# A Hymba block with PEER experts: the squares of the attention summed block by block, the conv squares added before one product, two 1/rms on quarters of the tokens

## The chip, the core and the metric

The kernel runs on one core of one Trainium2 chip. A core has a matrix engine (TensorE, PE), a vector engine (VectorE, DVE), a scalar engine (ScalarE, ACT), a general engine (GpSimd, POOL) and SyncE (SP), whose queue issues most DMA transfers. Each engine works through its own list of instructions in a fixed order; semaphores hold an instruction back until what it needs is done. The metric is the device time of one execution in microseconds (us), the median of several runs.

## The reference

One decoder layer over 512 tokens of width 1024, cut to what matters here:

```python
mod = c_act @ ada_w + ada_b                  # shift1, scale1, gate1, shift2, scale2, gate2
h = modulate(rmsnorm(x, norm1_g), shift1, scale1)
q, k, v, cb, cc, cu = split(h @ w_in)
attn = sliding_window_attention(rope(rmsnorm(q)), rope(rmsnorm(k)), v, sinks)   # 8 heads of 64
conv = cb * short_conv(cc * cu, conv_w)                                         # 512 channels
merged = concatenate([rmsnorm(attn, attn_out_g), rmsnorm(conv, conv_out_g)])
x = x + gate1 * (merged @ w_out)
h2 = modulate(rmsnorm(x, norm2_g), shift2, scale2)
x = x + gate2 * peer(h2, wq, subkeys, u, v)  # 16 queries per token, top 16 of 128 x 128 keys, 16384 experts
```

Each rmsnorm divides by the root of the mean square over the channels of one token. There are three such norms of whole rows that matter here: of the attention output (512 channels), of the conv output (512 channels), and of the new x ahead of PEER (1024 channels).

## The kernel before

Activations lie transposed: channels on the 128 partitions, in 8 chunks of 128, and the 512 tokens along the row. A product in full precision is made of three fast ones: each operand is split into a rounded part and a rest (`split`, lines 174 to 177: ACT copies the rounded part, hi, and DVE subtracts it for the rest, lo), and `mm3` (lines 197 to 202) multiplies hi by hi, hi by the activations' rest, and lo by hi. A block of 128 output channels over 1024 inputs is 24 products of 128x128 by 128x512.

The stages follow each other: the first norm and the modulation weights (0 to 60 us in the trace), the input projection with the attention and conv woven in (60 to 166), the rest of the attention (to 187), the output projection (to 231), the second norm and the first queries (to 254), the other queries (to 345), their routing and the table of the dense experts (to 640), and the experts themselves (to the end). PEER handles most tokens densely, with all 16384 expert rows streamed through, and the last ones by gathers of rows.

The order of the second stage is written out by hand in the string PLAN: A0 to A3 are the scores and softmax of four blocks of 128 tokens (`attend1`, line 374), B0 to B3 their second halves (`attend2`, lines 408 to 434: per head a transpose of the probabilities on PE, line 416, a copy pT on ACT, line 418, the products po, line 425; at the end of the block one copy into attnT, line 434), C30 to C32 the three projections of a conv chunk (lines 438 to 452), S the squares of the conv output summed by PE against a matrix of ones (lines 234 to 237), N the conv half of the merged norm (`part_norm`, lines 463 to 468: f is the scaled chunk on DVE, mH and mL its two parts), M two loads of modulation weights. The end of PLAN is "C31 C32 S B2 N B3 M M M". Behind it come the squares of attnT (ssa), the first half of the output projection for four blocks (py, over the conv half), the attention half of the norm, and the rest of the projection. A scheduler places the instructions on each engine, in about this order but by its own estimates of when they are ready.

Three details are needed below. A sum against ones gives the same sum on all 128 partitions, as a 128x512 tile in PSUM; `rstd` (lines 239 to 243) takes its root on ACT and the reciprocal on DVE, both 128x512. Modulation weights (`ada`, lines 204 to 214) are loaded into two buffers, each load held back until a mark on PE, and each multiplied and summed by one DVE instruction (junk, line 213). Temporary tiles come from one pool, tp, with nine buffers (line 107).

After the projection, `spill` (lines 528 to 536) transposes the new x by token (xt, 32 transposes on PE), copies it (xn on ACT, from pool rt with three buffers), and stores it to DRAM (x1s). The second norm's sums (ss2, lines 550 to 552) are one product over seven added squares and one over the eighth. The first two queries (pq) follow each chunk of the normed fH and fL (lines 226 to 232). Then pools are closed, and `query` (lines 721 to 732) loads its keys sk over SP's queue, into a pool opened on memory that tp gave back, and `scores` (lines 734 to 745) multiplies query and keys (psc).

Of the kernel before, what the change touches and what calls it, by code (L numbers as in the profile page):

```python
# [7 lines left out]
F32 = mybir.dt.float32  # L8
# [10 lines left out]
P = 128  # L19
# [70 lines left out]
def body(tc, p):  # L90
# [13 lines left out]
    rt, rt_s = pool("rt", side="right")  # L104
    R2 = dict(tag="s2", bufs=3)
    tp, tp_s = pool("tp", side="right")
    T2 = dict(tag="t2", bufs=9)
    xp, xp_s = pool("xp", side="right")

    def bank(name):  # L110
        return psm.tile([P, 512], F32, tag="m", name=name)
# [104 lines left out]
    def tmp(name):  # L216
        return tp.tile([P, T], F32, name=name, **T2)

    def squared(b, so_far=None):
        q = tmp("sq")  # L220
        nc.scalar.activation(q, b, AF.Square)
        if so_far is not None:
            nc.vector.tensor_add(q, q, so_far)
        return q
# [9 lines left out]
    def square(ps, b, i, n, w=None):  # L234
        q = tmp("sq")
        nc.scalar.activation(q, b, AF.Square)
        nc.tensor.matmul(ps, ones if w is None else w, q, start=(i == 0), stop=(i == n - 1))

    def rstd(ps, n):
        r = tmp("rstd")  # L240
        nc.scalar.activation(r, ps, AF.Sqrt, scale=1.0 / n, bias=eps)
        nc.vector.reciprocal(r, r)
        return r
# [130 lines left out]
    def attend1(n):  # L374
        k0 = 0 if n else P
        s = a1.tile([P, 8, 256], F32, tag="s", name="s", bufs=2)
        for b2 in range(2):
            pss = [bank("sc") for g in range(2)]
            for i in range(2):
                b = 2 * b2 + i  # L380
                for g, ps in enumerate(pss):
                    gp = slice(64 * g, 64 * g + 64)
                    nc.tensor.matmul(ps[:, i * 256 + k0:(i + 1) * 256], qT[gp, b, n * P:(n + 1) * P],
                                     kT[gp, (n - 1) * P + k0:(n + 1) * P], start=True, stop=True)
            for g, ps in enumerate(pss):
                for i in range(2):
                    h = 4 * g + 2 * b2 + i
                    nc.vector.scalar_tensor_tensor(s[:, h, k0:], ps[:, i * 256 + k0:(i + 1) * 256], rq[:, n, h:h + 1],
                                                   mask[:, k0:], op0=OP.mult, op1=OP.add)
        m = a1.tile([P, 8], F32, name="m", bufs=2)  # L390
        nc.vector.reduce_max(m, s[:, :, k0:], axis=X)
        nc.vector.tensor_max(m, m, S("sink"))
        nm = a1.tile([P, 8], F32, name="nm", bufs=2)
        nc.vector.tensor_scalar_mul(nm, m, -1.0)
        den = a1.tile([P, 8], F32, name="den", bufs=2)
        for h in range(8):
            nc.scalar.activation(s[:, h, k0:], s[:, h, k0:], AF.Exp, bias=nm[:, h:h + 1],
                                 accum_out=den[:, h:h + 1])
        es_ = a1.tile([P, 8], F32, name="es_", bufs=2)
        nc.vector.tensor_add(es_, S("sink"), nm)  # L400
        nc.scalar.activation(es_, es_, AF.Exp)
        nc.vector.tensor_add(den, den, es_)
        nc.vector.reciprocal(den, den)
        for h in range(8):
            nc.vector.tensor_scalar_mul(s[:, h, k0:], s[:, h, k0:], den[:, h:h + 1])
        return s
# [53 lines left out]
    vT = tmp("vT")  # L460
    nc.scalar.activation(vT, pj[5], AF.Copy)
    kg = S("kg")
    def part_norm(ss, src, g, o):
        r = rstd(ss, 512)
        for k in range(4):
            f = tmp("f")
            nc.vector.scalar_tensor_tensor(f, src[:, k, :], S(g, k), r, op0=OP.mult, op1=OP.mult)
            split(mH[:, o + k, :], mL[:, o + k, :], f)
# [4 lines left out]
    def out_half(b, half):  # L473
        if half == 0:
            wo[b] = weights_of(p["w_out"][b])
            py[b] = bank("py")
        mm3(py[b], wo[b], mh, ml, range(4 * half, 4 * half + 4))
# [3 lines left out]
    for step in PLAN.split():  # L481
        n = [int(x) for x in step[1:]]
        match step[0]:
            case "k":
                nk = qk1(pj[4], qk0(pj[4]), kg)
            case "q":
                nq[n[0]] = q0(pj[n[0]], n[0])
            case "P":
                pj[n[0]] = proj(n[0])
            case "V":  # L490
                pt = bank("vt")
                for c in range(NCH):
                    nc.tensor.transpose(pt[:, c * P:(c + 1) * P], vT[:, c * P:(c + 1) * P], ident)
                nc.scalar.activation(vN.rearrange("p a b -> p (a b)"), pt, AF.Copy)
            case "r":
                qk2(nq.pop(n[0]), qT[:, n[0], :])
            case "R":
                qk2(nk, kT)
            case "T":
                nc.scalar.activation(rq, ssq, AF.Sqrt, bias=eps64)  # L500
                nc.vector.reciprocal(rq, rq)
            case "A":
                sa[n[0]] = attend1(n[0])
            case "B":
                attend2(n[0], sa[n[0]])
            case "C":
                conv(*n)
            case "M":
                more_ada()
            case "S":  # L510
                ssc = bank("ssc")
                for k in range(4):
                    square(ssc, convT[:, k, :], k, 4)
            case "N":
                mH = a1.tile([P, DC, T], F32R, tag="hH", name="mH")
                mL = a1.tile([P, DC, T], F32R, tag="hL", name="mL")
                part_norm(ssc, convT, "cg", 0)
    ssa = bank("ssa")
    for k in range(4):
        square(ssa, attnT[:, k, :], k, 4)  # L520
    for b in range(HEAD):
        out_half(b, 0)
    part_norm(ssa, attnT, "ag", 4)
    ab = S("ada_b")
    nc.vector.tensor_add(mod[:, 16:24], mod[:, 16:24], ab[:, 16:24])
    x1s = dp.tile([NCH, P, D], F32, name="x1s")
# [1 line left out]
    def spill(half, when):  # L528
        for c in range(NCH):
            ps = bank("xt")  # L530
            for i in range(4):
                after(nc.tensor.transpose(ps[:, i * P:(i + 1) * P], xT[:, 4 * half + i, c * P:(c + 1) * P], ident),
                      when)
            xn = rt.tile([P, 512], F32, name="xn", **R2)
            nc.scalar.activation(xn, ps, AF.Copy)
            nc.sync.dma_start(x1s[c][:, half * 512:(half + 1) * 512], xn)

# [10 lines left out]
        if b < 6:  # L548
            more_ada(3)
    sq = squared(xT[:, 6, :], sq)  # L550
    nc.tensor.matmul(ss2, ones, sq, start=True, stop=False)
    end = nc.tensor.matmul(ss2, ones, squared(xT[:, 7, :]), start=False, stop=True)
    nc.vector.tensor_add(mod[:, 24:48], mod[:, 24:48], ab[:, 24:48])
    nc.vector.scalar_tensor_tensor(s2, mod[:, 32:40], 1.0, S("n2g"), op0=OP.add, op1=OP.mult)
    a1_s.close()
# [16 lines left out]
    hx, hx_s = pool("hx")  # L572
    fH = hx.tile([P, DC, T], F32R, name="fH")
    fL = hx.tile([P, DC, T], F32R, name="fL")
    r2 = rstd(ss2, D)
    spill(0, end)
    spill(1, end)
    early = [(weights_of(p["wq"][b]), bank("pq")) for b in range(EARLY)]
    fs = []
# [552 lines left out]
```

## Time and profile before

| | |
|---|---|
| three runs, us | 1436.77, 1436.56, 1435.25; median 1436.56 |
| the profiled execution, us | 1436.58 |
| its span in the trace, us | 1434.8 |
| PE busy | 1385.5 us, 97% of the span |
| DVE busy | 1229.3 us, 86% |
| ACT busy | 616.0 us, 43% |
| POOL busy | 442.7 us, 31% |
| mean granted clock of PE | 0.994 |

Times in the trace count from the start of the span. A row of the timeline has the start, the time from there to the end of the last of the group, the engine, the line of the kernel, the operation, out<-in, the shape and how many; in brackets stands the idle time just before it and what ended it. A fp32 product counts as two records. A line of the windows has the busy time of each engine in a stretch. "SPq" is a transfer's issue on SP's queue, not the transfer.

### The profile page before, as it was taken

To read this page: it belongs to the slowest core of one execution; us is meant where nothing else is said; L and a number is where in the kernel's file an instruction comes from. 1 tells how busy PE (TensorE), PEld (TensorE's weight loads), DVE (VectorE), ACT (ScalarE), POOL (GpSimd) and SP (SyncE) were. 2 spreads that over 40 slices of the span, in tenths; PEclk is the share of its full clock that TensorE was granted. 3 is DMA by queue.
4 is the path that set the end of the run, shared out by engine and by line. 5 is a ranking of instruction groups with operands and counts; after the bars stand their busy time and mean duration, and the time that the engine had idled before them with its cause. 6 is when DMAs were issued, how large, how long until landed. Compare 5 with 4: busy or idle time off the path is not lost.

```text
span 1434.8 us, 21241 instructions
## 1 busy us (share of the span) xinstructions
PE 1385.5 (97%) x7696; PEld 1218.7 (85%) x7696; DVE 1229.3 (86%) x2253; ACT 616.0 (43%) x1041; POOL 442.7 (31%) x306
## 2 busy tenths in 40 slices
PE   6999998999997999999999999999999999999998
PEld 4676776888997999999888888889999998889997
DVE  7778988789999999997668989888889979898964
ACT  4524645544634556463433333333344324333431
POOL 0000001440112320510134444456556556565400
PEclk9999999999999999999999999999999999999999
DMA  8645545322687997998999999999999999999843
GB/s 282 213 150 195 190 131 197 99 86 78 212 290 236 383 372 262 348 356 324 365 333 374 405 396 379 396 370 360 360 362 396 383 357 343 367 339 390 318 147 132
DMA packets 134376, 418.80 MB, mean 292 GB/s; under 512 B 12800, under 2 KB 39552, under 8 KB 132736
## 3 DMA queue, kind: packets, MB, share of 16 engines
q1 hardware_dynamic: 92800, 266.45, 51.6%
q0 software_dynamic: 41472, 151.01, 27.9%
q8 instruction: 60, 0.98, 0.3%
q14 instruction: 44, 0.36, 0.1%
HBM read 375.77 MB, written 41.62 MB: 291 GB/s over the span
## 4 chain that ended last, share of the span: by engine, by line
PE 62%; DVE 20%; DMA 8%; issue 7%; POOL 1%; ACT 1%; SPq 0%; DVEq 0%; POOLq 0%; ACTq 0%
PE o L997 10%; PE o L998 10%; PE o L996 10%; PE pa L200 5%; PE pa L202 5%; PE pa L201 5%; DVE lo L177 4%; DMA row<-in_vL,eG 3%; DMA ada<-in_ada 2%; PE pq L202 2%; PE pq L201 2%; PE pq L200 2%; DVE B L946 2%; DVE ga L912 2%; PE pj L200 2%
## 5 line engine op out<-in xcount | busy, mean ns | idle before, releaser
L176 ACT ACTIVATE hi<-raw 128x1024 fp32r<-128x1024 f32 x298 | 312.1, 1053 | 286.8 <-issue 91.4
L177 DVE TENSOR_TENSOR lo<-raw,hi 128x1024 fp32r<-128x1024 f32 x284 | 345.2, 1218 | 31.9 <-ACT hi L176 31.1
L202 PE MATMUL pa<-h2H,lo 128*128 128x352 f32 x1024 | 329.8, 322 | 5.6 <-DVE lo L177 5.5
L200 PE MATMUL pa<-h2H,hi 128*128 128x352 f32 x1024 | 332.3, 325 | 2.2 <-ACT sp L620 2.2
L201 PE MATMUL pa<-h2L,hi 128*128 128x352 f32 x1024 | 328.9, 321 | 0.0
L997 PE MATMUL o<-lo,wwh 128*128 128x512 f32 x768 | 299.2, 390 | 0.9 <-DVE lo L177 0.9
L996 PE MATMUL o<-hi,wwh 128*128 128x512 f32 x768 | 299.6, 390 | 0.0
L998 PE MATMUL o<-hi,wwl 128*128 128x512 f32 x768 | 298.8, 389 | 0.0
L776 POOL DMA_INDIRECT row<-in_uR,eG x128 | 186.7, 1459 | 321.3 <-PE o L998 187.8
L776 POOL DMA_INDIRECT row<-in_vL,eG x128 | 178.8, 1397 | 136.8 <-PE o L998 65.6
L784 DVE SCALAR_TENSOR_TENSOR junk<-row,h2N 128x1024 bf16<-128x1024 f32 x128 | 153.8, 1220 | 64.9 <-DMA row<-in_uR,eG 64.4
L202 PEld LDWEIGHTS pa<-h2H,lo 128*128 128x128 f32 x1024 | 192.7, 188 | 6.9 <-DVE lo L177 6.8
L200 PEld LDWEIGHTS pa<-h2H,hi 128*128 128x128 f32 x1024 | 192.2, 188 | 4.9 <-ACT sp L620 2.7
L201 PEld LDWEIGHTS pa<-h2L,hi 128*128 128x128 f32 x1024 | 192.5, 188 | 2.2
L912 DVE SCALAR_TENSOR_TENSOR ga<-row,av,ga 128x1024 f32<-128x1024 f32 x127 | 162.8, 1282 | 29.8 <-DMA row<-in_vL,eG 28.7
L998 PEld LDWEIGHTS o<-hi,wwl 128*128 128x128 f32 x768 | 144.2, 188 | 30.0
L997 PEld LDWEIGHTS o<-lo,wwh 128*128 128x128 f32 x768 | 144.2, 188 | 29.7 <-DVE lo L177 1.6
L996 PEld LDWEIGHTS o<-hi,wwh 128*128 128x128 f32 x768 | 144.2, 188 | 28.3 <-issue 0.2
L176 ACT ACTIVATE wwh<-w 128x768 fp32r<-128x768 f32 x64 | 54.1, 846 | 168.0 <-DVE w L979 120.8
L177 POOL TENSOR_TENSOR lo<-raw,hi 128x1024 fp32r<-128x1024 f32 x14 | 33.8, 2413 | 288.3 <-ACT hi L176 288.3
L978 ACT ACTIVATE w<-G 128x32 f32<-128x32 f32 x128 | 22.3, 221 | 191.3 <-DVE wwl L177 182.8
L776 POOL DMA_INDIRECT row<-in_uR,eH x32 | 43.2, 1350 | 161.7 <-DVE junk L784 74.5
(266 smaller groups left out, 1896.1 us busy)
## 6 DMA issues: line engine op xcount, KB each, us to landing
raw<-in_uL SPq DMA_DIRECT2D x128, 512.0 KB, 6.0
raw<-in_vL SPq DMA_DIRECT2D x128, 512.0 KB, 6.5
Gd<-st SPq DMA_DIRECT2D x12, 2048.0 KB, 10.2
G<-Gd SPq DMA_DIRECT2D x16, 1536.0 KB, 12.5
ada<-in_ada SPq DMA_DIRECT2D x32, 512.0 KB, 4.3
Ad<-sp SPq DMA_DIRECT2D x34, 352.0 KB, 6.5
sp<-Ad SPq DMA_DIRECT2D x34, 352.0 KB, 6.6
raw<-in_w_in SPq DMA_DIRECT2D x18, 512.0 KB, 5.2
```

Of the source, the lines that this page charges most:

```text
L176: nc.scalar.activation(h, f, AF.Copy)
L177: by.tensor_sub(l, f, h.bitcast(F32))
L200: nc.tensor.matmul(ps, wh(k), rh(k), start=(k == k0), stop=False)
L201: nc.tensor.matmul(ps, wh(k), rl(k), start=False, stop=False)
L202: mark[0] = nc.tensor.matmul(ps, wl(k), rh(k), start=False, stop=(k == k1))
L776: d = nc.gpsimd.indirect_dma_start(out=t, out_offset=None, in_=tab, in_offset=bass.IndirectOffsetOnAxis(ap=e, axis=0))
L784: return nc.vector.scalar_tensor_tensor(junk, t, 1.0, h, op0=OP.mult, op1=OP.mult, accum_out=a)
L912: nc.vector.scalar_tensor_tensor(ga, t, av[:, k:k + 1], ga, op0=OP.mult, op1=OP.add)
L946: nc.vector.tensor_mul(B.rearrange("p t (h a b) -> p t h a b", h=8, a=4), H[:, ts, :, None, :].to_broadcast(sh), L[:, ts, None].to_broadca ...
L996: nc.tensor.matmul(o, wh[:, cs], vh[:, hs], start=(j == 0), stop=False)
L997: nc.tensor.matmul(o, wh[:, cs], vl[:, hs], start=False, stop=False)
L998: last = nc.tensor.matmul(o, wl[:, cs], vh[:, hs], start=False, stop=(j == NJ - 1))
```

## The change

Four things change.

- **The attention's squares.** As soon as the copy of a token block into attnT is there, its squares are taken (`attn_squares`) and summed by four products with 32 columns of ones into 32 partitions: block 0 and 1 after A3, block 2 in step N, ahead of the conv norm, and block 3 behind the first half of block 0 of the output projection. The root and the reciprocal are then taken on a 128x128 tile (four groups of 32 partitions, one for each block of 128 tokens; `grouped_root`), and `spread` brings the result back to 128x512 with four products.
- **The conv squares** are added on DVE first, and one product sums them.
- **The second norm** has its sums in the same grouped form: two times four products, a 128x128 root and reciprocal, and `spread` between the two halves of the transposes.
- **Buffers.** tp has 13 buffers where it had 9, and xn comes from it.

```diff
-    T2 = dict(tag="t2", bufs=9)
+    T2 = dict(tag="t2", bufs=13)
...
+    def grouped(ps, q, first, last):
+        for c in range(NCH):
+            end = nc.tensor.matmul(ps[32 * c:32 * c + 32, 0:P], ones[:, 0:32], q[:, c * P:(c + 1) * P], start=first,
+                                   stop=last)
+        return end
+    def grouped_root(ps, n):
+        r = cp.tile([P, P], F32, tag="r", name="r", bufs=1)
+        nc.scalar.activation(r, ps[:, 0:P], AF.Sqrt, scale=1.0 / n, bias=eps)
+        nc.vector.reciprocal(r, r)
+        return r
+    def spread(r):
+        ps = psa.tile([P, 512], F32, tag="a", name="rr")
+        for c in range(NCH):
+            nc.tensor.matmul(ps[:, c * P:(c + 1) * P], ident[:, 32 * c:32 * c + 1].to_broadcast([P, P]), r,
+                             start=True, stop=True)
+        return ps
...
+    def attn_squares(n):
+        if n == 0:
+            ssa.append(psa.tile([P, 512], F32, tag="a", name="ssa"))
+        q = tmp("sq").rearrange("p (k t) -> p k t", k=4)
+        nc.scalar.activation(q, attnT[:, :, n * P:(n + 1) * P], AF.Square)
+        for k in range(4):
+            nc.tensor.matmul(ssa[0][32 * n:32 * n + 32, 0:P], ones[:, 0:32], q[:, k], start=(k == 0), stop=(k == 3))
...
             case "A":
                 sa[n[0]] = attend1(n[0])
+                if n[0] == NCH - 1:
+                    for c in range(NCH - 2):
+                        attn_squares(c)
...
             case "S":
                 ssc = bank("ssc")
+                q = None
                 for k in range(4):
-                    square(ssc, convT[:, k, :], k, 4)
+                    q = squared(convT[:, k, :], q)
+                nc.tensor.matmul(ssc, ones, q, start=True, stop=True)
             case "N":
...
-                part_norm(ssc, convT, "cg", 0)
-    ssa = bank("ssa")
-    for k in range(4):
-        square(ssa, attnT[:, k, :], k, 4)
-    for b in range(HEAD):
+                attn_squares(NCH - 2)
+                part_norm(rstd(ssc, 512), convT, "cg", 0)
+    out_half(0, 0)
+    attn_squares(NCH - 1)
+    ra = grouped_root(ssa[0], 512)
+    for b in range(1, HEAD):
         out_half(b, 0)
-    part_norm(ssa, attnT, "ag", 4)
+        if b == 1:
+            ra = spread(ra)
+    part_norm(ra, attnT, "ag", 4)
...
-            xn = rt.tile([P, 512], F32, name="xn", **R2)
+            xn = tmp("xn")
...
-    nc.tensor.matmul(ss2, ones, sq, start=True, stop=False)
-    end = nc.tensor.matmul(ss2, ones, squared(xT[:, 7, :]), start=False, stop=True)
+    grouped(ss2, sq, True, False)
+    end = grouped(ss2, squared(xT[:, 7, :]), False, True)
...
-    r2 = rstd(ss2, D)
+    r2 = grouped_root(ss2, D)
     spill(0, end)
+    r2 = spread(r2)
     spill(1, end)
```

What the scheduler makes of it is seen in the order of each engine. On DVE, ahead of the output projection, before (convT is the last conv chunk, lo the rest of a weight block, junk the modulation weights, rstd the reciprocal of the conv norm, f its first scaled chunks):

```order
L177 TENSOR_TENSOR lo<-raw,hi 128x1024
L452 TENSOR_TENSOR convT<-pj,y 128x512
L177 TENSOR_TENSOR lo<-raw,hi 128x1024
L213 SCALAR_TENSOR_TENSOR junk,mod<-ada,cact 128x1024 x2
L242 RECIPROCAL rstd<-rstd 128x512
L213 SCALAR_TENSOR_TENSOR junk,mod<-ada,cact 128x1024
L467 SCALAR_TENSOR_TENSOR f<-convT,sm,rstd 128x512 x3
```

and now, where sq<-sq adds the squares of the conv chunks:

```order
L223 TENSOR_TENSOR sq<-sq 128x512
L473 TENSOR_TENSOR convT<-pj,y 128x512
L223 TENSOR_TENSOR sq<-sq 128x512
L177 TENSOR_TENSOR lo<-raw,hi 128x1024
L223 TENSOR_TENSOR sq<-sq 128x512
L213 SCALAR_TENSOR_TENSOR junk,mod<-ada,cact 128x1024
L177 TENSOR_TENSOR lo<-raw,hi 128x1024
L213 SCALAR_TENSOR_TENSOR junk,mod<-ada,cact 128x1024 x4
L263 RECIPROCAL rstd<-rstd 128x512
L213 SCALAR_TENSOR_TENSOR junk,mod<-ada,cact 128x1024
L498 SCALAR_TENSOR_TENSOR f<-convT,sm,rstd 128x512 x3
```

The reciprocal of the conv norm stood behind two junk operations and now stands behind five; the last sum of squares stands behind a weight split. On ACT at the same place, before (pT are the copies of the transposed probabilities, the first eight of block B2, and rstd<-ssc the root of the conv norm):

```order
L236 ACTIVATE sq<-convT 128x512
L418 ACTIVATE pT<-pT 128x256 x3
L241 ACT_TABLE_LOAD
L241 ACTIVATE rstd<-ssc,eps 128x512
L418 ACTIVATE pT<-pT 128x256 x5
L434 ACTIVATE attnT<-po 128x4x128
```

and now:

```order
L221 ACTIVATE sq<-convT 128x512
L439 ACTIVATE pT<-pT 128x256 x8
L455 ACTIVATE attnT<-po 128x4x128
L439 ACTIVATE pT<-pT 128x256
L491 ACTIVATE sq<-attnT 128x512
L262 ACT_TABLE_LOAD
L262 ACTIVATE rstd<-ssc,eps 128x512
```

The root moved from behind the third pT copy of B2 to behind all of B2, one copy of B3 and the square of token block 2. On SP's queue, between the stores of x1 and the queries, before (x1s<-xn stores x1, sk are the keys of a query, raw<-in_wq a block of query weights):

```order
L536 DMA x1s<-xn 128x512 x8
L729 DMA sk<-in_sk 128x128 x3
L181 DMA raw<-in_wq 128x1024
L729 DMA sk<-in_sk 128x128
L181 DMA raw<-in_wq 128x1024
```

and now:

```order
L575 DMA x1s<-xn 128x512 x8
L181 DMA raw<-in_wq 128x1024
L769 DMA sk<-in_sk 128x128 x3
L181 DMA raw<-in_wq 128x1024
L769 DMA sk<-in_sk 128x128 x2
```

A load of query weights moved ahead of the first three loads of keys. It waits for POOL's split (lo) of an earlier block, before as now. The first sk load now also waits for the seven other transfers' queues, for DVE and for PE, since its buffer lies on memory that tp's larger ring held; before, it waited for DVE, PE and one transfer's queue.

On PE, eight of the small products for the squares now stand ahead of the last conv chunk's projection; the single product of the conv squares stands ahead of B2's transposes; the squares of the last token block stand behind block 0's first half of the output projection, the four products of `spread` behind block 1's; and in the second norm the order is 16 transposes, four products of `spread`, 16 transposes. On ACT all eight xn copies now stand ahead of the first fH; before, five did. The scores of query 0 stand ahead of the products of the third query, before as now.

More of the change, by code (lines that the diff above doesn't have):

```diff
@@ L462, in body, with part_norm @@
     kg = S("kg")
-    def part_norm(ss, src, g, o):
-        r = rstd(ss, 512)
+    ssa = []
+    def attn_squares(n):
[5 more added lines that the diff above has]
+            nc.tensor.matmul(ssa[0][32 * n:32 * n + 32, 0:P], ones[:, 0:32], q[:, k], start=(k == 0), stop=(k == 3))
+    def part_norm(r, src, g, o):
         for k in range(4):
```

## The prediction

> **What bounds the kernel now.** I read the page first, for the span, and then the busy times by window, for the stages that the change touches and two behind them. Their columns are the window, its length, busy time and instructions of TensorE (PE), of its weight loads, of VectorE (DVE), ScalarE (ACT) and GpSimd (POOL), the granted TensorE clock, and the DMA share.
>
> ```profile
> span 1434.8 us, 21241 instructions
> ...
> 166.00:187.00 21.00, 17.30 (x113) 10.28 (x113) 18.64 (x27) 13.84 (x30) 0.00 (x0) 1.00 0.61 201
> ...
> 187.00:231.00 44.00, 44.00 (x194) 36.05 (x192) 36.40 (x49) 14.46 (x18) 2.60 (x1) 1.00 0.51 165
> ...
> 254.00:345.00 91.00, 91.00 (x464) 77.01 (x462) 79.93 (x496) 37.74 (x78) 28.43 (x12) 1.00 0.32 97
> ...
> 400.00:640.00 240.00, 229.06 (x1894) 224.97 (x1894) 239.44 (x469) 122.61 (x212) 60.90 (x40) 0.99 0.88 322
> ```
>
> The output projection (187 to 231) and the queries (254 to 345) leave PE no gap; from 400 to 640 DVE has none (239.44 of 240). So a delay at 187 or at 254 should travel whole to the end. What can be won or lost lies between: 3.7 us without PE in 166 to 187, and the second norm after 231. The PE timeline shows who ends those gaps.
>
> ```profile
> 136.81 1.09 PE L416 MATMUL pT<-cst,s 128*128 128x128 f32 x8
> ...
> 142.40 2.00 PE L383 MATMUL sc<-kT,qT 64*128 64x256 f32 x16
> ...
> 166.06 0.39 PE L202 MATMUL pj<-hH,lo 128*128 128x512 f32 x1
> ...
> 179.38 1.31 PE L425 MATMUL po<-pT,vN 128*64 128x128 f32 x16
> ...
> 183.50 1.98 PE L237 MATMUL ssa<-sq,ones 128*128 128x512 f32 x4 [2.80 <-ACT sq L236]
> 185.77 1.98 PE L237 MATMUL ssa<-sq,ones 128*128 128x512 f32 x4 [0.29 <-ACT sq L236]
> 187.19 0.80 PE L200 MATMUL py<-mH,hi 128*128 128x512 f32 x1
> ...
> 230.93 0.39 PE L202 MATMUL py<-mH,lo 128*128 128x512 f32 x1
> ```
>
> The in-projection ends at 166.45. Before py, PE has 2.80 + 0.29 us idle, waiting for the attention's last copy and squares, and four long products; the conv norm (mH) is ready by then. This is what the change is aimed at. Block B1 takes 5.6 us of PE (136.81 to 142.40). From 187.19 to 230.93 a product starts every (43.74 - 0.64)/190 = 0.227 us.
>
> **The change, part by part: up to the output projection.** The small products have no row of their own. The nearest are po (16 records, eight products, 1.31 us: 0.16 each) and psc (in the fence on the tail; four products, the next one starts 0.82 later: 0.21 each). I take 0.2, with 0.15 as the lower end. Eight of them now stand ahead of the last four projection blocks, which so end at 166.45 + 1.6 = 168.1.
>
> ```profile
> 173.11 1.23 DVE L213 SCALAR_TENSOR_TENSOR junk<-ada,cact 128x1024 bf16<-128x1024 f32 x1 [2.35 <-DMA ada<-in_ada]
> 175.48 3.35 DVE L242 RECIPROCAL rstd<-rstd 128x512 f32<-128x512 f32 x1
> ...
> 179.99 2.07 DVE L467 SCALAR_TENSOR_TENSOR f<-convT,sm,rstd 128x512 f32<-128x512 f32 x3
> 181.98 1.89 DVE L177 TENSOR_TENSOR mL<-f,mH 128x512 fp32r<-128x512 f32 x3
> ```
>
> The conv squares are now added on DVE, three adds of about 0.65 (the time of mL or f), and one product follows the last add. In the new order that add stands behind the last convT and one weight split: 168.1, convT and an add to 169.6, the split (1.23 on the same width) and an add to 171.4. B2's transposes stand behind that product on PE, so PE idles from 168.1 to 171.4, 3.3 us; it runs the product to 172.3, and B2 to 177.9.
>
> On ACT the root of the conv norm now stands behind eight pT copies, attnT, another pT and a square of attnT:
>
> ```profile
> 171.13 1.28 ACT L241 ACT_TABLE_LOAD   x1
> ...
> 176.10 1.21 ACT L418 ACTIVATE pT<-pT 128x256 f32<-128x256 f32 x4
> ```
>
> pT is 0.3 each, attnT and a square 0.6 each, the table load 1.28: 177.9 + 0.6 + 0.3 + 0.6 + 1.3 + 0.6 puts the root at 181.2. Two later pT copies wait behind it, so B3 ends near 185.
>
> The reciprocal meets a longer wait on DVE, since five junk operations (products with the modulation weights, ada) stand ahead of it where two stood. ada has two buffers, so each load is issued after the junk two before it. The landing times of the two loads at 166.5 and of the three from 174.4:
>
> ```profile
> L211 SPq DMA_DIRECT2D ada<-in_ada x2: 327/379/431, 166.5 to 166.8; - x2
> ...
> DMA to landing us min/median/max: 6.6/7.0/7.5
> ```
> ```profile
> L211 SPq DMA_DIRECT2D ada<-in_ada x3: 327/328/328, 174.4 to 180.1; - x3
> ...
> DMA to landing us min/median/max: 3.4/4.4/4.8
> ```
>
> The first pair waits for the last projection product, 168.1, as it did at 166.48. I give the first load 3.4 (the weight loads ahead of it have 1.6 us more to clear), the next 4.4, the third 3.4. First load lands at 171.5, its junk ends at 172.8; the third load of the stage goes out at 172.9, lands at 177.3, junk to 178.5; the fifth goes out at 178.6, lands at 182.0, junk to 183.2. Then the reciprocal, 3.35, to 186.6, one more junk to 187.8, the first f to 188.5 and mH (some 0.65) to 189.1. So py starts near 189.2, with PE idle for about 4 us after B3. The first block is then paced by DVE: f x3 and mL x3 to 191.8, f, mH and mL to 193.6; 179 products remain at 0.227 (40.6), and eight small ones for the last squares and the spread of 1/rms (1.6). The last py starts at 235.8 against 230.93: **+4.9**. With all loads at 3.4 and 0.15 a small product it is +3.1; with 6.6, 4.8 and 4.4 it is +9.5.
>
> [...]
>
> **The change, part by part: the tail.** Times here are in before's frame, without the 4.9.
>
> ```profile
> 234.08 1.12 PE L552 MATMUL ss<-sq,ones 128*128 128x512 f32 x2 [0.20 <-ACT sq L221]
> 235.04 3.66 PE L532 MATMUL xt<-cst,xT 128*128 128x128 f32 x32
> ...
> 241.74 0.73 PE L200 MATMUL pq<-fH,hi 128*128 128x512 f32 x2 [3.04 <-ACT fH L230]
> ...
> 253.19 1.91 PE L593 MATMUL pg<-cst,f 128*128 128x128 f32 x16
> 254.93 1.06 PE L738 MATMUL psc<-sk,qs 128*128 128x128 f32 x8
> ```
> ```profile
> 235.96 3.35 DVE L242 RECIPROCAL rstd<-rstd 128x512 f32<-128x512 f32 x1 [2.45 <-ACT rstd L241]
> ```
> ```profile
> 240.97 0.71 ACT L230 ACTIVATE fH<-f,mod 128x512 fp32r<-128x512 f32 x1
> ```
>
> A 128x128 reciprocal is no row; by width it is 3.35/4 = 0.84, with the full 3.35 as the other end. Grouped products end at 234.9, root 235.3, reciprocal 236.2, ready before half the xt transposes are through (236.9). The four spreading products (0.8) then fill PE till 237.5, and the other half runs to 239.4. But ACT now copies all eight xn before the first fH, and the last xn ends at about 239.95; fH starts at 240.0 against 240.97, and the first queries come some 1.1 earlier: pq's last product ends near 252 where it ended at 253.19. With the full 3.35 the spread waits until 238.7 and this 1.1 is gone.
>
> What is late next is the key load sk of query 0. The larger tmp pool pushes the pool that holds sk down onto buffers of tmp, so sk now waits for their last readers, the last of them PE's pg transposes; and on SP's queue the load of in_wq, which waits for POOL's lo, stands ahead of it.
>
> ```profile
> 253.60 2.37 POOL L177 TENSOR_TENSOR lo<-raw,hi 128x1024 fp32r<-128x1024 f32 x1 [18.26 <-ACT hi L176]
> ```
> ```profile
> 249.27 1.28 SPq L729 DMA_DIRECT2D sk<-in_sk  x3
> ...
> 256.00 0.33 SPq L181 DMA_DIRECT2D raw<-in_wq  x1
> ```
> ```profile
> L729 SPq DMA_DIRECT2D sk<-in_sk x10: 328/328/423, 249.3 to 294.4; - x10
> ...
> DMA to landing us min/median/max: 1.7/1.8/3.3
> ```
>
> These are ten sk loads. The 3.3 belongs to the one issued at 256.43, right behind the load of in_wq at 256.00; that is where the first will now stand, so I take it, and 1.7 as the other end. Before, sk went out at 249.27, 5.7 us before psc. Now: POOL's lo 1.1 earlier, in_wq out at 254.9, sk at 255.3, landed at 258.6; psc, which stands ahead of the third query's products on PE, starts at 258.7 against 254.93: **+3.7**, with PE idle 5.0 us. If sk lands in 1.7 it is +2.1.
>
> **The clock.** The gaps of 2.80 and 3.04 us above left the granted clock at 1.00. The one longer gap in the first part of the dense build:
>
> ```profile
> 444.66 0.27 PE L954 MATMUL gps<-B,A 128*128 128x128 f16 x1 [6.99 <-DVE B L946]
> ```
> ```profile
> 441.00:442.00 1.00, 0.00 (x0) 0.85 0.53 57
> ...
> 447.00:448.00 1.00, 1.00 (x13) 0.50 0.36 61
> 448.00:449.00 1.00, 1.00 (x13) 0.73 0.75 213
> ```
>
> It fell about 4.2 us into the gap (0.50 from about 441.8) and came back near 448.5, so 3.8 us of work ran at half, at most 1.9 lost. The gap of 5.0 us before psc is longer than 4.2, the other two are not. I take half of it, **+0.9**, with 0 and 1.9 as ends. [...]
>
> **Sum.** 4.9 + 3.7 + 0.9 = +9.5 on the profiled execution. That took 1436.58, 1.78 around its span of 1434.8, and is the median of the runs shown: 1446.1. The ends of the terms give 3.1 + 2.1 = 5.2 (1441.8) and 9.5 + 3.7 + 1.9 = 15.1 (1451.7).
>
> **The rivals.** *More lost:* the clock falls after all three new gaps (3.3, 4 and 5.0). For it: all three are longer than any that kept the clock. Against: the fall came 4.2 into the gap. Three times 1.9 on 8.6 is 14.3: 1450.9.
>
> *The lost time is made up later, so no slower.* DVE sets the pace from 400 to 640, and has 11 us free from 254 to 345. If its work there keeps its old pace and only PE's start slips, PE's delay is taken out of the 11 us that PE idles in the dense build. Deciding point: whether the last DVE operation before 345 starts later. Then all but about 0.5 returns: 1437. Against: DVE's work there follows each psc.
>
> *The saving comes through, so faster.* If the ada weights land early enough that the reciprocal has ended when B3 ends (reciprocal started by 181.8 at the latest), py starts at 185.2, 2.0 earlier, less 1.6 for the eight small products; the tail's 1.1 comes on top if sk is not late: 1435.1; a little more if the small products take 0.15, and a first block without pauses. Against: three chained loads that each take at least 3.4.
>
> **How the numbers follow.** Forecast 0.74, all of it slower; more lost 0.08, slower; made up later 0.09, the same; the saving 0.09, of which 0.05 faster and 0.04 the same. Same means within 0.2%, 2.9 us, about what a measurement of this kernel can tell from no change. So 0.05, 0.13 and 0.82. The range holds the forecast and the first rival, from 1440.0 (the lower end 1441.8, less the 1.3 by which the fastest run lay under the median, and a little for grouped products that may run side by side) to 1451.7; 0.18 is left below.
>
> **What would show it.** PE idle at 168 to 171 with DVE's add as releaser; DVE waiting for ada three times ahead of the reciprocal, which starts near 183; the first py near 189; 1/rms of the second norm ready before the ninth xt group; psc waiting for the sk load, with about 5 us of PE idle. I am wrong if py starts before 187, if psc waits less than 2 us, or if the stages after 345 don't keep the delay.

## The result and the profile after

The changed kernel takes 1453.37 us (median of four runs, 1450.05 to 1455.28) against 1436.66 for the kernel before: a ratio of 1.0114, with a 95% interval of 1.0092 to 1.0136. It is slower, as forecast, by 16.7 us where 9.5 were forecast, and 1.7 above the end of the range. Run once more among the experiments it came to 1.0106 (1.0072 to 1.0140). The profiled execution is the slowest of the first four, 1455.28, 18.7 above before's, so its terms add up to more than the median shows.

Where the time comes from is read first from PE's timeline, whose gaps stand in brackets.

```profile
168.61 0.39 PE L202 MATMUL pj<-hH,lo 128*128 128x512 f32 x1
...
172.64 1.13 PE L549 MATMUL ssc<-sq,ones 128*128 128x512 f32 x2 [3.63 <-DVE sq L223]
...
190.97 1.65 PE L200 MATMUL py<-mH,hi 128*128 128x512 f32 x3 [4.12 <-ACT mH L176]
...
238.33 0.39 PE L202 MATMUL py<-mH,lo 128*128 128x512 f32 x1
239.94 0.43 PE L242 MATMUL ss<-sq,ones 128*32 128x128 f32 x8 [1.22 <-DVE sq L223]
241.26 0.42 PE L242 MATMUL ss<-sq,ones 128*32 128x128 f32 x8 [0.90 <-ACT sq L221]
241.62 3.46 PE L571 MATMUL xt<-cst,xT 128*128 128x128 f32 x16
244.87 1.27 PE L256 MATMUL rr<-r,cst 128*128 128x128 f32 x8
...
249.33 0.73 PE L200 MATMUL pq<-fH,hi 128*128 128x512 f32 x2 [1.45 <-ACT fH L230]
...
260.89 1.80 PE L633 MATMUL pg<-cst,f 128*128 128x128 f32 x15
267.86 2.05 PE L778 MATMUL psc<-sk,qs 128*128 128x128 f32 x8 [5.16 <-DMA sk<-in_sk]
```

The three forecast gaps are there: 3.63 (3.3 forecast), 4.12 (4) and 5.16 (5.0), with the releasers that were named. The last py starts at 238.33 against 230.93, the first scores at 267.86 against 254.93. The 16 transposes of 241.62 are slow, which wasn't forecast: they take 3.3 us where 1.8 were expected. The granted clock in the windows of one us says why (columns: busy time of PE, clock, DMA share, GB/s).

```profile
174.00:175.00 1.00, 1.00 (x6) 0.50 0.89 311
...
191.00:192.00 1.00, 1.00 (x3) 0.50 0.00 0
...
243.00:244.00 1.00, 1.00 (x6) 0.50 0.61 57
...
270.00:271.00 1.00, 1.00 (x4) 0.50 0.89 352
```

The clock fell four times between 166 and 275, where before it had stayed at 1.00: from about 173.6 to 177.0, 190.7 to 194.1, 241.9 to 245.3, and 265.8 to 272.6. The chain ahead of py is on DVE:

```profile
178.36 1.23 DVE L213 SCALAR_TENSOR_TENSOR junk<-ada,cact 128x1024 bf16<-128x1024 f32 x1 [2.28 <-DMA ada<-in_ada]
...
181.31 1.22 DVE L213 SCALAR_TENSOR_TENSOR junk<-ada,cact 128x1024 bf16<-128x1024 f32 x1 [1.71 <-DMA ada<-in_ada]
...
184.00 1.23 DVE L213 SCALAR_TENSOR_TENSOR junk<-ada,cact 128x1024 bf16<-128x1024 f32 x1 [1.46 <-DMA ada<-in_ada]
...
185.15 3.35 DVE L263 RECIPROCAL rstd<-rstd 128x512 f32<-128x512 f32 x1
```

Three waits for modulation weights stand ahead of the reciprocal, as the order of DVE said. On SP's queue the keys go out behind the query weights:

```profile
263.69 0.33 SPq L181 DMA_DIRECT2D raw<-in_wq  x1
264.33 1.28 SPq L769 DMA_DIRECT2D sk<-in_sk  x3
```

### The profile page after: what moved, and what is told of

The parts are those of the page before. It is cut to its first block, busy times and chain, and to the rows that moved or that the text cites. A ratio compares the mean times of both kernels' runs of the same rounds, so it can differ in the third digit from the quotient of the medians.

```text
span 1453.5 us, 21336 instructions
## 1 busy us (share of the span) xinstructions
PE 1395.6 (96%) x7742; PEld 1229.9 (85%) x7742; DVE 1226.7 (84%) x2256; ACT 617.4 (42%) x1041; POOL 443.9 (31%) x306
## 4 chain that ended last, share of the span: by engine, by line
PE 51%; DVE 20%; DMA 12%; issue 11%; POOL 5%; ACT 1%; SPq 0%; POOLq 0%; DVEq 0%; ACTq 0%
PE pa L202 7%; PE pa L200 7%; PE pa L201 6%; PE o L1038 5%; PE o L1036 5%; PE o L1037 5%; DMA row<-in_uR,eG 5%; POOL row L816 5%; DVE lo L177 4%; DMA ada<-in_ada 3%; DMA row<-in_vL,eG 2%; DVE junk L824 2%; PE pq L201 2%; PE pq L202 2%; DVE B L986 2%
## 5 line engine op out<-in xcount | busy, mean ns | idle before, releaser
L816 POOL DMA_INDIRECT row<-in_uR,eG x128 | 190.6, 1489 | 320.6 <-PE o L1038 182.3
L201 PEld LDWEIGHTS pa<-h2L,hi 128*128 128x128 f32 x1024 | 193.3, 189 | 2.2
```

The source lines that it names most:

```text
L201: nc.tensor.matmul(ps, wh(k), rl(k), start=False, stop=False)
L816: d = nc.gpsimd.indirect_dma_start(out=t, out_offset=None, in_=tab, in_offset=bass.IndirectOffsetOnAxis(ap=e, axis=0))
```

## The experiments

Single runs of one kernel differ by several us: 25 runs of the kernel before lay between 1432.8 and 1442.6, and 30 others between 1432.5 and 1447.0. Part of that stands in the traces. The last projection product started between 163.8 and 169.1 in the profiled executions, also in kernels whose instructions up to there are the same, and the granted clock between 120 and 130 differed too: 0.83 in the kernel before, 0.71 in the changed one, 0.67 to 0.88 in e1 to e4. So kernels are compared by their ratios, and the causes by stages. The table has the time in us from each point on PE to the next, from the starts of first and last instructions: last projection product, first py, last py, first query product (pq), first scores (psc), last query product, first product of the dense build (gps).

| kernel | to py | to last py | to pq | to psc | to last pq | to gps | ratio to before |
|---|---|---|---|---|---|---|---|
| before | 21.1 | 43.7 | 10.8 | 13.2 | 89.4 | 100.3 | |
| changed | 22.4 | 47.4 | 11.0 | 18.5 | 91.7 | 101.5 | 1.0114 |
| changed, again (e5) | 22.4 | 48.2 | 8.3 | 18.4 | 92.3 | 101.9 | 1.0106 |
| nine buffers (e1) | 22.4 | 47.5 | 8.3 | 16.6 | 89.4 | 100.5 | 1.0058 |
| root first (e2) | 17.6 | 46.4 | 8.3 | 18.5 | 90.8 | 101.5 | 1.0052 |
| scores gap filled (e3) | 22.2 | 47.4 | 11.2 | 18.7 | 89.4 | 101.6 | 1.0052 |
| the same again (e10) | 22.4 | 47.4 | 8.3 | 18.6 | 89.4 | 100.9 | 1.0068 |
| norm gap filled (e4) | 22.9 | 48.4 | 9.4 | 18.5 | 91.7 | 101.9 | 1.0110 |
| root first, keys apart (e6) | 17.5 | 46.4 | 8.3 | 14.8 | 89.5 | 101.9 | 1.0008 |
| also conv on PE (e7) | 14.8 | 46.9 | 11.2 | 14.8 | 89.5 | 101.8 | 0.9992 |
| second norm only (e8) | 21.6 | 43.7 | 9.3 | 14.8 | 89.5 | 101.2 | 1.0003 |
| copies in own buffers (e9) | 14.8 | 46.9 | 9.9 | 13.2 | 89.4 | 101.5 | 0.9982 |
| 13 buffers only (e11) | 21.8 | 43.7 | 8.7 | 21.0 | 91.2 | 100.4 | 1.0047 |

My theory was that the loss is the sum of these waits and of the half clocks behind them. The rivals were that the dense build takes part of it back, that single waits only hide others, and that the half clock costs nothing by itself.

**The buffers.**

```diff
-    T2 = dict(tag="t2", bufs=13)
+    T2 = dict(tag="t2", bufs=9)
```

> The changed kernel with nine tmp buffers again in place of 13 (xn stays in tmp). The sk loads then stand ahead of the load of in_wq on SP's queue and wait for nothing late. Theory (the sk wait of 5.2 us and the clock fall of about 2.3 us that follows it are a part of the loss by themselves): PE starts the scores of query 0 right behind pg, no 5 us gap, no half clock at that place, 7.5 us less than the changed kernel, about 1446. Rival (the time lost at the scores is made up later by the dense stage, so removing it gives nothing): less than 2 us, about 1452.

It came to 1446.05, a ratio of 1.0058 (1.0037 to 1.0079). PE's timeline:

```profile
261.60 1.80 PE L633 MATMUL pg<-cst,f 128*128 128x128 f32 x15
263.23 1.06 PE L778 MATMUL psc<-sk,qs 128*128 128x128 f32 x8
```

The scores follow pg without a gap and at full clock, and the scores and the products behind them take 89.4 us again, as before. So the sk wait and its half clock are a part of the loss by themselves, and the dense build behind them does not make it good: it takes as long as in every other run. But that the kernel came out at the 1446 of the theory is in part luck, since the smaller ring brings a wait of its own. DVE's scaled chunks f lie in that ring, and now wait until the copies xn have been stored; PE then waits for DVE among the first query products.

```profile
247.10 1.41 DVE L229 SCALAR_TENSOR_TENSOR f<-xT,s,rr 128x512 f32<-128x512 f32 x2 [2.90 <-DMA x1s<-xn]
```
```profile
249.23 0.55 PE L201 MATMUL pq<-fL,hi 128*128 128x512 f32 x1 [1.89 <-DVE fL L231]
```

The clock fell there too (0.50 from 250 to 251), so the stretch to the scores takes 16.6 and not 13.2. To the scores, and from there to the last query product, the kernel has 1.9 and 2.3 us less than the changed one, 4.2 and not 7.5. Another 2.7 of its profiled run lie in the second norm, and they do not come from the buffers, as is shown below.

**The order on ACT and DVE.**

```diff
+                rc = rstd(ssc, 512)
                 attn_squares(NCH - 2)
-                part_norm(rstd(ssc, 512), convT, "cg", 0)
+                part_norm(rc, convT, "cg", 0)
```

> The changed kernel with the root of the conv norm written ahead of the square of token block 2. On ACT the root then stands ahead of B2's copies, on DVE the reciprocal behind three junk operations where five stood. Theory (the reciprocal behind two more chained loads makes py late): the reciprocal starts near 179.6 where it started at 185.15, py near 187 where it started at 190.97; 3.5 to 4.5 us less, about 1449. Rival (the root on ACT was the late one, or B3's end is next): the reciprocal moves but py moves by less than 2 us.

The ratio was 1.0052 (1.0033 to 1.0071), 1445.36. The last projection product started at 166.00 in this run. DVE and PE:

```profile
176.13 1.23 DVE L213 SCALAR_TENSOR_TENSOR junk<-ada,cact 128x1024 bf16<-128x1024 f32 x1 [2.67 <-DMA ada<-in_ada]
...
177.28 3.35 DVE L263 RECIPROCAL rstd<-rstd 128x512 f32<-128x512 f32 x1
```
```profile
182.67 0.87 PE L446 MATMUL po<-pT,vN 128*64 128x128 f32 x10
183.57 0.73 PE L200 MATMUL py<-mH,hi 128*128 128x512 f32 x2
184.24 0.65 PE L446 MATMUL po<-pT,vN 128*64 128x128 f32 x6
```

One chained load instead of three, the reciprocal 5 us earlier counted from the projection's end, and py starts before B3 is through: 4.8 us less to the first py, as the theory had it and a little more, and 1.0 less from there to the last py. The order of two statements in the source decided this. The kernel as a whole came out 8.0 below the changed one, more than these stages explain; 2.7 of its profiled run lie in the second norm, as in the run with nine buffers.

**The half clocks.** 20 products were put into the gap ahead of the first scores, in a bank that the scores overwrite:

```diff
         pc = bank("psc")
+        if hp == 0:
+            for i in range(20):
+                nc.tensor.matmul(pc, fH[:, 0, 0:P], fH[:, 1, :], start=True, stop=True)
```

> The changed kernel with 20 more products in PE's gap ahead of the first scores; they write a bank that the scores then overwrite, so nothing of the result depends on them. The sk wait stays. Theory (the clock fall costs by itself): no half clock from 266 to 272, the scores and the first seven products behind them at full speed, 2.3 us less than the changed kernel at that place, about 1451. Rival (the clock is only recorded lower, or the loss is made up): no change, and the scores take 2 us as before.

```profile
259.67 4.82 PE L779 MATMUL psc<-fH 128*128 128x512 f32 x20
265.19 1.13 PE L781 MATMUL psc<-sk,qs 128*128 128x128 f32 x8 [0.70 <-DMA sk<-in_sk]
```

The wait for sk is as long as before, but the scores take 1.13 where they took 2.05, and the stretch to the last query product is 89.4 instead of 91.7: 2.2 us, as forecast. The whole kernel came out lower than that explains, 1446.34 (1.0052, interval 1.0031 to 1.0074), so both kernels were run again:

> The changed kernel with PE's gap ahead of the first scores filled, once more: its first runs came out 7 us below the changed kernel, of which its trace explains 2.3 (the half clock) and 3 lie in the stretch from the dense build to the first product of the experts, which differs from run to run. Theory (only the half clock is saved): 1449 to 1451. Rival (the half clock costs more later on): 1446.

> The changed kernel once more, beside the others of this call, since single runs of one kernel differ by several us. Theory (the loss is the sum of the waits and half clocks that its profile shows, 15.2 us by the first scores, and little more): 1451 to 1454. Rival (its first four runs were slow by chance, and the half clock ahead of the scores costs much less than the 7 us by which the kernel with that gap filled came out lower): 1447 to 1449.

The filled kernel came to 1447.40 (1.0068, 1.0046 to 1.0090), the changed one to 1452.53 (1.0106, 1.0072 to 1.0140): the first between its theory and its rival, the second inside the range of its theory. At that place 2.2 to 2.8 us are shown by the stages; the ratios differ by 0.4 to 0.6%, some 5 to 9 us, with intervals wide enough for 3. What the rest is, if there is one, stays open.

In the second norm, two times four products were put around the first grouped sums:

```diff
+    wf = psa.tile([P, 512], F32, tag="a", name="wf")
+    for i in range(8):
+        if i == 4:
+            grouped(ss2, sq, True, False)
+        after(nc.tensor.matmul(wf, mH[:, 0, 0:P], mH[:, 1, :], start=True, stop=True), mark[0])
-    grouped(ss2, sq, True, False)
```

> The changed kernel with two times four more products around the first sums of the second norm, where PE idled 1.2 and 0.9 us; they write a bank that is not read. Theory (the short grouped sums left PE so little to do that the clock fell, which slowed the 16 transposes and delayed the spread): no half clock from 242 to 245, the first 16 transposes in 1.8 us where they took 3.3, and the first query product about 1.4 us earlier after the last py. Rival (ACT's copies and the reciprocal set the pace there): the first query product moves by less than 0.5 us.

```profile
240.66 1.07 PE L594 MATMUL wf<-mH 128*128 128x512 f32 x4
241.98 0.42 PE L242 MATMUL ss<-sq,ones 128*32 128x128 f32 x8 [0.26 <-DVE sq L223]
242.34 1.20 PE L594 MATMUL wf<-mH 128*128 128x512 f32 x4
243.46 0.42 PE L242 MATMUL ss<-sq,ones 128*32 128x128 f32 x8
243.82 1.97 PE L571 MATMUL xt<-cst,xT 128*128 128x128 f32 x16
```

The clock held (1.00 from 238 to 255), the transposes took 1.97, and the first query product came 9.4 behind the last py instead of 11.0. But this does not show that the filling held the clock, and the whole kernel was no faster, 1454.17 (1.0110, 1.0072 to 1.0147). What PE idles here is decided ahead of it, by a small instruction of DVE, the modulation weights s of 128x8. In the profiled run of the changed kernel it took 2.39 us:

```profile
234.31 2.39 DVE L593 SCALAR_TENSOR_TENSOR s<-mod,sm 128x8 f32<-128x8 f32 x1
```

POOL's split of a weight block had begun 0.03 us ahead of it and took 2.39 too. In five of the thirteen profiles s began behind that split, took 2.36 to 2.39 and ended within 0.04 us of it; in the other eight it began ahead of it and took 0.16. Why it waits so isn't shown; that it does decides the stretch. Of the ten kernels with the grouped sums and no filling in the norm, the four where s took 2.4 have both gaps of PE, 1.2 to 1.5 and 0.9 us, and take 11.0 to 11.2 where the clock fell (changed, e3, e7) and 9.3 where it held (e8). The six where it took 0.16 have one gap of 1.15 us and no fall, and take 8.3, or 9.9 where the copies wait for their stores (e9). The filled kernel is one with 0.16: without the filling 8.3 is what such a run takes. So the fall cost 1.7 here (11.0 less 9.3), the late s 1.0, and this experiment leaves open whether the filling would have saved the former. The order in which two engines arrive differs from run to run of the same kernel, as the changed kernel's two profiles show, and gives or takes 2.7 us. The grouped form itself is worth less: with an early s and the larger ring it takes 8.3 (e5), the old form 8.7 (e11).

**Both causes taken away.** To the root first came the key buffers in another pool:

```diff
-        sk = rp.tile([P, P], F32, tag="sk", name="sk", bufs=3)
+        sk = hx.tile([P, P], F32, tag="sk", name="sk", bufs=3)
```

> The changed kernel with both causes taken away: the root of the conv norm ahead of token block 2's square, and the key buffers in the pool that holds fH, so that the sk loads wait for nothing of tmp. Theory: py starts some 17 us after the last projection product (before: 20.7), the second norm takes 8.0 from the last py to the first query product (before: 10.4) where the clock holds, and the scores follow pg without a gap; the out-projection carries 1.6 more small products, so 3.4 us less than the kernel before, about 1434, and 19 less than the changed one. Rival (a next wait takes their place, or the dense stage takes the gain back): 1437 or more.

It counts from the end of a product, 0.4 behind the start that the table uses, and so does the one for the second norm below. The result was 1440.45, a ratio of 1.0008 (0.9989 to 1.0027): the loss is gone, but the 3.4 us of gain did not come. The rival was right, and the profile names the next wait, on PE and then on DVE:

```profile
250.29 1.80 PE L634 MATMUL pg<-cst,f 128*128 128x128 f32 x15
253.50 1.16 PE L779 MATMUL psc<-sk,qs 128*128 128x128 f32 x8 [1.41 <-ACT qs L772]
```
```profile
255.68 0.49 DVE L668 MAX8 V<-scd 128x8 f32<-128x128 f32 x2 [7.53 <-ACT scd L781]
```

qs, ACT's copy of query 0, lies in a pool opened on memory of tmp's larger ring too, and ACT's order has it behind four copies of pg. The scores come 14.8 behind the first query product where it was 13.2, and DVE's routing starts 5.4 us behind the first pg where it was 3.7 before (256.87 less 253.19), by DVE's timeline of the kernel before:

```profile
256.87 0.49 DVE L627 MAX8 V<-scd 128x8 f32<-128x128 f32 x2 [5.79 <-ACT scd L740]
```

The wait on ACT is longer by about as much as the scores are late, and the routing starts from there. Another 1.6 us of the gain were lost on the way to the dense build, and the late routing isn't shown to be the cause: in e9, below, it starts 3.7 behind pg as before and this stretch still takes 101.5, and in e11 it starts 10.1 behind and the stretch takes 100.4.

**The conv squares.** The same kernel with four products instead of the adds:

```diff
-                    q = squared(convT[:, k, :], q)
-                nc.tensor.matmul(ssc, ones, q, start=True, stop=True)
+                    square(ssc, convT[:, k, :], k, 4)
```

> As the kernel with root first and keys apart, but the conv squares are again four products on PE with no adds on DVE. Theory (PE's gap of 3.7 us behind the projection and its half clock lie in the shadow of the weight loads and the reciprocal, which set py): within 1 us of that kernel. Rival (the adds and the gap cost by themselves): 1.5 to 3 us less than it, about 1432.

1437.45, 0.9992 (0.9972 to 1.0012), 3 us below the last one, though the intervals overlap. The stages show 2.1 us from the last projection product to the last py (61.8 against 63.9), since PE's gap is gone and the root of the conv norm starts sooner. With the root first, nothing shadows the gap any more: by the stages my theory falls here, and the rival holds.

**The second norm only.** Of the change only its grouped sums and the buffers are left, with the keys apart:

> Of the change only the second norm's grouped sums, the buffers and xn in tmp, with the key buffers in the pool that holds fH; attention and conv squares are as before. Theory: 8.0 to 9.2 us from the last py to the first query product where it was 10.4, so 1.2 to 2.4 less than the kernel before, about 1435. Rival (the short sums let the clock fall here, and the grouped form gives nothing): no change, 1437.

1437.67, 1.0003 (0.9979 to 1.0028). 1.5 us came off the stretch to pq and 1.6 were added in the next one by the late qs: no difference.

**The buffers only.** The kernel before with the 13 tmp buffers and xn in tmp:

> The kernel before with only the 13 tmp buffers and xn in tmp; all squares and norms as before. Theory (the buffers alone make the sk wait of some 5 us, the half clock behind it, and the late copy qs): PE idle some 5 us ahead of the first scores, 7 to 9 us more than the kernel before, about 1446. Rival (the wait comes only with the changed norm's timing): less than 2 us.

```profile
251.48 1.91 PE L624 MATMUL pg<-cst,f 128*128 128x128 f32 x16
259.01 2.04 PE L769 MATMUL psc<-sk,qs 128*128 128x128 f32 x8 [5.62 <-DMA sk<-in_sk]
```

1443.55, 1.0047 (1.0025 to 1.0068), 6.9 us above the kernel before. The larger ring with xn in it, and nothing else of the change, makes the sk wait of 5.62 us and the scores at half clock (2.04).

**What comes out a little below the kernel before.** Root first, conv squares on PE, nine tmp buffers, keys where they were, and the copies xn in buffers of the pool that holds fH:

```diff
-            xn = tmp("xn")
+            xn = hx.tile([P, 512], F32, tag="xn", name="xn", bufs=6)
```

> As the kernel with root first and conv squares on PE, but nine tmp buffers as before, keys where they were before, and the xn copies in six buffers of the pool that holds fH. On ACT the copy qs of query 0 then stands ahead of the hN copies again. Theory (the tmp ring of 13 costs 1.6 us ahead of the first scores and 1.3 ahead of the dense build, since pools opened later lie on it): 61.8 us from the last projection product to the last py (before: 64.8), 8.3 to 9.7 to the first query product (10.8), 13.2 to the scores and 100.4 from the last query product to the first product of the build, as before; less 1.6 for the small products, so 2.5 to 4 us less than the kernel before. Rival (the gains in the early stages are made good by waits later, whatever the buffers): no difference from the kernel before.

```profile
247.90 1.91 PE L632 MATMUL pg<-cst,f 128*128 128x128 f32 x16
249.65 1.06 PE L777 MATMUL psc<-sk,qs 128*128 128x128 f32 x8
```

1434.42 against 1436.69, a ratio of 0.9982 (0.9967 to 0.9997): 2.3 us between the medians, a little less than the 2.5 to 4 expected, and with an interval that barely leaves out no difference. It has 61.7 to the last py (64.9 before) and 13.2 to the scores, and by the stages 2.9 less from the last projection product to the dense build. The 101.5 to the dense build didn't become 100.4, and the kernel with the 13 buffers alone has 100.4: that part of my expectation, that the ring costs 1.3 there, falls, and what moves this stretch between 100.3 and 101.9 isn't known.

## Why the prediction was wrong

The order of the mechanisms was right, and the direction. The sum was too small, and the step that failed is **the clock**: 0.9 was put for one fall that might come. In the profiled run two falls cost 2.3 us behind the scores and 1.7 in the second norm, and a third goes with 2.4 us between the dense build and the experts. Of the 18.7 us that this run is slower, 9.2 were not forecast; 5.5 of them lie there, the 2.4 by argument alone.

- **To the first py:** forecast 189.2, with the projection's last product starting at 167.7, so 21.5; measured 22.4. The reciprocal began 16.5 us behind that start, where 15.5 was forecast, since the fifth modulation load took about 4.4 where 3.4 was put. **To the last py:** 46.6 forecast, 47.4 measured. Both terms together were 1.6 too small; another 0.9 of the +7.4 at the last py is the early part of that one run.
- **The second norm:** forecast -1.1 (by the rows it was worked out from, fH at 240.0 and 240.97, it should have been -1.0). Measured +0.2 in the profiled run and -2.5 in five others. Of the working, the reciprocal on 128x128 took 0.95 (0.84 forecast), and the spread came before the second half of the transposes, as written. What I left out was the fall of the clock, 1.7, and that DVE's s can come late or not: the kernel before was profiled with the late s, 2.36 us. The little that the range's lower end took off for grouped products side by side had no row behind it; the runs show four products for four groups of 32 partitions in 0.42 to 0.43 us, and four for one group in 1.06.
- **The sk wait:** from the last run of pg products to the scores 7.0 us where it was 1.7, 5.2 more; forecast 3.7 + 1.1. Right.
- **The clock:** I had drawn a line at a gap of 4.2 us from one row, and that row gives 4.0 (PE idle from 437.67, half clock from 441.7). The mistake is the line itself: the clock fell after gaps of 3.63 and 4.12 here and behind two of 2.21 and 0.49 at the first query products of e11 (products 0.43 us apart from there to 242.0, then 0.23), and held after 3.07 ahead of pq in e9 (0.23 apart). The last section has what the runs show of it. The fall behind the scores cost 2.3 (91.7 less 89.4), the one in the second norm 1.7. The two ahead of py cost nothing that shows in this run, as DVE set the pace there: the product of 195.49 waited for mL, which ended at 195.43. In e5 the products behind the second gap started 0.43 us apart from the first py, at 187.58, to 193.3, for 5.7 us where it was 3.1 here, and the stretch to the last py took 48.2 instead of 47.4, so there it did cost about 0.8. The rival that had named three falls came nearest with 1450.9, but for another reason than it gave: of its three falls one cost something here, and so did one that it did not name.
- **After the queries:** forecast nothing more or less. The dense build passed the delay on whole (200.4 us or 200.5 in all thirteen profiles), so that the delay made up later was wrong. 1.2 more were lost on the way to it, by a cause that isn't known.
- **Between the dense build and the first expert product:** forecast nothing; 43.7 us where it was 41.3. In five profiles this stretch goes with the clock: it takes 41.3 before and 40.8 in e11, with a clock of 1.00 from 660 to 710, but 43.7 in the changed kernel, with half clock from 692.4 to 695.9, and 43.3 in e5 and 42.4 in e10, both with a mean of 0.97. Over all thirteen it lies between 40.4 and 44.9. No run changes the clock there alone, so the cause is argued.
- **The saving that comes through** failed at the point that was named, the chained loads. With the root first it comes: 17.6 to py against 21.1.

For the profiled run the terms by stages, unrounded, add up to 13.9: 1.2 + 3.6 + 0.2 + 5.3 + 2.3 + 1.2. To them come 2.5 at the end of the projection (the eight small products there take some 1.5, forecast 1.6; the rest is put down to the early clock, 0.71 between 120 and 130 where it was 0.83) and the 2.4 ahead of the experts: 18.8, of 18.7 measured.

## What to carry to other kernels

When a change makes a ring of buffers larger, look at what is opened later on the same memory: a load that was free to go early may now wait for the last reader of a buffer that it has nothing to do with (here PE idled 5.16 us for the keys), and so may every instruction that writes there. Where a scheduler sets the order, a statement put ahead of another by habit can move a root behind eight copies and a reciprocal behind three loads; read the order of the engine that waits before costing the arithmetic. And a gap on PE costs more than its length when the clock falls behind it (here 2.3 us on top of the 5.16), so a change that only makes PE's work shorter ahead of a wait may give its gain back. Before such a gain or loss is put down to an edit, look at the same stretch in a second profile of the same kernel: here the second norm differed by 2.7 us between two profiles of one kernel.

## What the runs showed of the hardware

In the changed kernel's profile, between 166 and 275, the half clock came in pieces, worked out from the windows of one us: 3.4 us after the gaps of 3.63 and 4.12 and in the second norm, and 6.8 after 5.16. It began 3.1 to 4.6 us after the start of the gap, once only when PE was at work again (the gap ended at 172.64, the clock fell at about 173.6).

The trace of the kernel before and that of the changed one can each be cut by their own changes of the clock: within each they all lie whole multiples of 3.41 us apart. From 160 us to the last 20, with the clock full in the stretch itself, it was half behind all seven stretches of that length in which PE was busy for 0.38 of it or less (one before, from 438.29, and six in the changed kernel), and behind none of the others, in which it was busy for 0.52 or more. Ahead of 160 us it also fell behind busier ones, of 0.82 (from 56.00) and 0.54 (from 117.44) before, of 0.92 (from 57.57) and 0.47 (from 115.60) in the changed kernel, so the busy share alone doesn't tell it. The same two gaps in the second norm, 1.22 and 0.90 us, fell differently into these stretches in the changed kernel, where the clock fell, and in e8, where it held: 0.38 and 0.49 of the stretch busy (columns: length, PE busy, clock, DMA share, GB/s):

```profile
238.48:241.89 3.41, 1.29 (x20) 1.00 0.84 300
```
```profile
228.77:232.18 3.41, 1.66 (x14) 1.00 0.60 183
```

The 128x128 reciprocal took 0.95 us where the 128x512 took 3.35. Four products of 128x32 that add up in the same 32 partitions, as in ssa, took 1.06 us; four that write four different groups of 32, as in ss, took 0.42 to 0.43. Between two py products, the four of ssa delay the second one more than the four 128x128 products of the spread do: 1.31 to 1.33 us from the start of the one py to the start of the other in the changed kernel, e2, e5 and e7, against 1.03 in the changed kernel, e5 and e7. Within both groups a record starts every 0.11 us, so the difference of about 0.3 us lies at the edges, where the shape changes from 128x128 to 128x32 and back; that the change of shape is its cause isn't shown.
